# A hybrid encoder block: gate sums in two tiles, q and k weights split by halves of a head's dims, ropes without transfers

## The chip, the cores and the metric

The kernel runs on one core of a Trainium2 chip. The metric is the time of one execution on the device in microseconds (us). One execution was also recorded by the hardware profiler. The engines are TensorE (PE, its weight loads PEld), VectorE (DVE), ScalarE (ACT), GpSimd (POOL) and SyncE (SP), which here only issues transfers.

## The reference

One encoder block on 1024 tokens of width 1024, all in float32:

```
h    = rms_norm(x)
proj = h @ w_in                        # 1024 x 5120
qa, ka, va, qb, kb, vb, ga, gb = split(proj)
qa, ka, qb, kb = apply_rope(each)      # heads of 64 dims
ya = dilated_window_attention(qa, ka, va) @ w_branch_a
yb = differential_attention(qb, kb, vb) @ w_branch_b
x  = x + (sigmoid(ga) * ya + sigmoid(gb) * yb) @ w_out
x  = x + square(relu(rms_norm(x) @ w_ff1)) @ w_ff2
out = rms_norm(x)

def apply_rope(t):                     # per head, halves t1, t2 of 32 dims
    rot = concat([-t2, t1])
    return t * cos + rot * sin
```

What is computed here is q, k and the gates: 16 columns of 128 outputs for q and k (j = 0 to 15, two heads of 64 dims each) and 16 for the gates, out of `proj`.

## The kernel before

**Products.** Every float32 operand is split into a high and a low part (`halves`, L245 on ACT for the high part, L246 on POOL for the low), and a product takes three matmuls per block of the contraction: high by high, high by low, low by high. The projections go by the Strassen-Winograd form of a 2x2 block product: 7 products instead of 8, each of 12 matmuls of 128x512 (`product`, L237), with sums on the weights before (`rest_operands`, L265 to L268 on VectorE) and sums on the results behind (`rest_products`, L286 to L298). The blocks of the activations (B11, B21, B22, T1 to T4) lie split in SBUF.

**Stage 0** (to about 142 us) normalises and transposes x, forms v, and computes for four q/k pairs the first two of the 7 products (`qk_early`, `EARLY = (8, 12, 10, 14)`), which are parked in DRAM.

**Stage 1** (about 142 to 428 us) runs 16 tasks one behind the other: q8 g4 q12 g5 q10 g6 q14 g7 q0 g0 q4 g1 q2 q6 g2 g3. A q task (`qk_pair(j)`) forms the columns j and j + 1, a g task (`gate_rest(n)`) three quarters of two gate columns. An early q task and every gate task have 5 products here, the late q tasks (0, 4, 2, 6) 7. The products of a task stand in this order: s2 and s4 (into the PSUM tile y), s1 and s3 (into z), a4 (into "4"). The raw weights of a task are loaded two tasks ahead on SyncE's queue, 512 KB a tile. From them come three pairs of split tiles: ws (halves s2 and s4 of the first raw tile), wd (s1) and wt (s3 and a4 of the second). They take turns in three buffers (tags wh and wl), so a task's ws goes into the buffer of the ws of the task before, and so on; a late q task takes one more for its first two products (wa).

**Results and the rope.** A q task's sums go into two tiles of 128x1024, raw j and raw j + 1, of a tag "x" with four buffers. A gate task's three sums (gc0, gc1, gc2) take three buffers of the same tag and are stored to DRAM from SyncE's queue (`part_d`, gp in the trace, L539). The rope of a pair is emitted one task later, for j and then j + 1:

```
for b in range(4):                      # L493: swap the halves, 4 copies of 128 KB
    nc.sync.dma_start(rot[32*b:32*b+32, :], raw[32*(b^1):32*(b^1)+32, :])
rot = rot * scale * sin_t               # L494 VectorE
raw = raw * cos_t                       # L495 POOL
raw = raw * scale + rot                 # L496 VectorE
hi  = copy(raw)                         # L504 ACT
lo  = raw - hi                          # L505 VectorE
nc.scalar.dma_start(qk_d[j][0], hi)     # L506, on ACT's queue
nc.scalar.dma_start(qk_d[j][1], lo)     # L507
```

The column of a q/k tile holds two heads on 128 partitions, so the two halves of a head lie on different partitions.

**Order.** The code only says what depends on what. A scheduler sets the order of the instructions on each engine, and each engine (and each queue) then runs its list in that order. A tile's buffer is given on when the last instruction or transfer that uses it has ended. Behind stage 1 the attention phase takes the buffers of stage 1's ropes for its loads (kb and qb in the trace, L662 and L668), and its first statement on VectorE is a memset (L918) of a tile that lies where gate sums lay.

Of the kernel before, what the change touches and what calls it, by code (L numbers as in the profile page):

```python
# [37 lines left out]
def shape_tables():  # L38
# [8 lines left out]
    sin_t = np.concatenate([-sin, sin, -sin, sin], 0)  # L47
# [36 lines left out]
def tile_hybrid_block(ctx: ExitStack, tc: tile.TileContext, t: dict, out: bass.AP):  # L84
# [92 lines left out]
    qk_d = [dram(f"qk{j}", [2, P, S]) for j in range(16)]  # L177
# [84 lines left out]
    def rest_operands(name, ra, rb, s1):  # L262

        a11, a12, a21, a22 = ra[:, :DK, :], ra[:, DK:, :], rb[:, :DK, :], rb[:, DK:, :]
# [3 lines left out]
        nc.vector.tensor_tensor(a12, a12, a11, op=ALU.subtract)  # L268
        s2, s4 = halves(ra, f"ws_{name}")
# [248 lines left out]
    def qk_pair(j, raws):  # L518
# [5 lines left out]
        else:  # L524
            a11, a12 = halves(raws[0], f"wa_q{j}")
# [944 lines left out]
```

## Time and profile before

| | |
|---|---|
| time, median of 3 runs | 1668.82 us (1664.23 to 1673.82) |
| profiled execution | 1674.86 us, span 1673.1 us |
| busy: PE / DVE / ACT / POOL | 1557.9 / 1181.4 / 697.6 / 585.3 us (93 / 71 / 42 / 35%) |
| TensorE's granted clock over the span | 0.972 of 2.4 GHz |
| SyncE's queue / ACT's queue | 236.33 / 33.56 MB |
| transfers inside the rope | 64 of 128 KB, median 4.5 us to landing |
| q/k stores | 32 of 512 KB, median 4.8 us to landing |

The clock has two levels, 1.2 GHz (0.5) and 2.4 GHz (1.0); a stretch's mean lies between. A wait is put down to the engine, DMA or queue that released it last. An idle time in brackets stands on the instruction that ended it. PE is the busiest engine, so a gap of PE is what a change can take away, and a gap of another engine costs only where PE waits behind it.

### The profile page before, as it was taken

Reading aid. Unit: us, or ns where it says so; the run is one execution under the profiler, and the core shown is the slowest. Engines: PE = TensorE matmul, PEld = TensorE weight load, DVE = VectorE, ACT = ScalarE, POOL = GpSimd, SP = SyncE. Lnnn points to the kernel's source line nnn. Section 1 sums busy time; section 2 is a strip of 40 time slices with the busy share of each in tenths; the row PEclk is TensorE's granted clock in tenths of the full one; section 3 lists DMA queues with packets and bytes.
Section 4 is the critical chain, followed back from the end, with each engine's and each line's share of the span. In section 5 each row is a group of like instructions: output and inputs, shape, how many; then the busy total and the mean of one; then the engine's idle time right before and its main releaser. Section 6 shows DMA issues by size and latency. Waiting matters only on the chain. (4 is left out here: it accounts for less than half of the span.)

```text
span 1673.1 us, 20932 instructions
## 1 busy us (share of the span) xinstructions
PE 1557.9 (93%) x7832; PEld 1299.2 (78%) x7832; DVE 1181.4 (71%) x1367; ACT 697.6 (42%) x1064; POOL 585.3 (35%) x289
## 2 busy tenths in 40 slices
PE   8899889988789998989999999899999989999998
PEld 6798667766577887988887878687888867888776
DVE  5976798698688996645547357644355599898984
ACT  4432122232467774544433236444444552333331
POOL 1534444555232332012220003533333344354551
PEclk8999899998999999999999999999999999999999
DMA  6367566555767557656557333444333571423112
GB/s 214 125 210 215 164 196 223 175 184 163 263 194 233 200 191 271 204 180 215 156 162 278 110 130 94 120 128 130 114 101 101 179 268 51 163 74 116 51 38 101
DMA packets 214389, 271.23 MB, mean 162 GB/s; under 512 B 12784, under 2 KB 136848, under 8 KB 214288
## 3 DMA queue, kind: packets, MB, share of 16 engines
q1 hardware_dynamic: 200464, 236.33, 44.4%
q10 hardware_dynamic: 13824, 33.56, 5.3%
q8 instruction: 62, 1.02, 0.3%
q14 instruction: 39, 0.32, 0.1%
HBM read 183.81 MB, written 80.27 MB: 158 GB/s over the span
## 5 line engine op out<-in xcount | busy, mean ns | idle before, releaser
L1359 PE MATMUL p<-b,a 128*128 128x512 f32 x392 | 154.7, 395 | 5.1 <-DVE b L1274 5.1
L1358 PE MATMUL p<-b,a 128*128 128x512 f32 x392 | 154.2, 393 | 3.0 <-ACT a L1273 3.0
L1360 PE MATMUL p<-b,a 128*128 128x512 f32 x392 | 154.4, 396 | 2.0 <-DVE a L1274 1.9
L1274 POOL TENSOR_TENSOR b<-ws,b 128x1024 fp32r<-128x1024 f32 x20 | 61.4, 3088 | 95.3 <-ACT b L1273 85.3
L1359 PEld LDWEIGHTS p<-b,a 128*128 128x128 f32 x392 | 74.2, 189 | 23.0 <-DVE b L1274 6.0
L1274 POOL TENSOR_TENSOR b<-rb,b 128x1024 fp32r<-128x1024 f32 x21 | 70.8, 3390 | 54.7 <-ACT b L1273 46.7
L1360 PEld LDWEIGHTS p<-b,a 128*128 128x128 f32 x392 | 74.0, 189 | 20.1 <-DVE a L1274 3.9
L1358 PEld LDWEIGHTS p<-b,a 128*128 128x128 f32 x392 | 74.1, 189 | 19.8 <-ACT a L1273 3.4
L689 PE MATMUL sb<-kb,qb 128*128 128x512 f32 x256 | 74.7, 416 | 15.1 <-ACT p L694 8.8
L694 ACT ACTIVATE p<-sb,mn 128x1024 f32<-128x1024 f32 x64 | 71.3, 1116 | 38.5 <-DVE mn L692 23.7
L692 DVE TENSOR_REDUCE mn<-sb 128x1 f32<-128x1024 f32 x64 | 76.8, 1217 | 9.7 <-PE sb L689 9.2
L265 DVE TENSOR_TENSOR s<-w 128x512 f32<-128x512 f32 x15 | 16.2, 1081 | 85.8 <-DMA w<-in_w_ff 85.8
L156 POOL TENSOR_SCALAR n_y<-n_ss 128x1 f32<-128x1 f32 x23 | 5.1, 222 | 187.7 <-ACT n_xn L163 183.2
L803 PE MATMUL sa<-kh_a,zq 128*128 128x256 f32 x256 | 68.9, 300 | 1.2 <-DVE mna L812 1.2
L828 DVE TENSOR_TENSOR pta<-ta,pta 128x512 fp32r<-128x512 f32 x64 | 43.8, 688 | 33.9 <-ACT pta L827 33.7
L689 PEld LDWEIGHTS sb<-kb,qb 128*128 128x128 f32 x256 | 45.9, 192 | 27.9 <-ACT p L694 13.1
L1273 ACT ACTIVATE a<-fs 128x1024 fp32r<-128x1024 f32 x28 | 29.4, 1054 | 90.6 <-PE p L1359 71.3
L803 PE MATMUL sa<-kl_a,zq 128*128 128x256 f32 x256 | 65.8, 288 | 0.0
L246 POOL TENSOR_TENSOR wt_f_l<-w,wt_f_h 128x1024 fp32r<-128x1024 f32 x15 | 36.1, 2404 | 83.0 <-ACT wt_f_h L245 70.2
L816 ACT ACTIVATE sm<-sm,mna 128x512 f32<-128x512 f32 x64 | 46.1, 720 | 32.4 <-DVE mna L812 31.8
L827 ACT ACTIVATE pta<-ta 128x512 fp32r<-128x512 f32 x64 | 37.6, 591 | 52.2 <-PE ta L823 44.5
L1145 ACT ACTIVATE c<-c 128x512 f32<-128x512 f32 x64 | 39.9, 624 | 46.6 <-DVE c L292 34.9
(442 smaller groups left out, 4966.4 us busy)
## 6 DMA issues: line engine op xcount, KB each, us to landing
w<-in_w_in SPq DMA_DIRECT2D x32, 512.0 KB, 4.3
qk<-r ACTq DMA_DIRECT2D x32, 512.0 KB, 4.8
f<-c ACTq DMA_DIRECT2D x64, 256.0 KB, 2.0
rb<-in_w_ff SPq DMA_DIRECT2D x32, 512.0 KB, 4.6
ra<-f SPq DMA_DIRECT2D x64, 256.0 KB, 5.0
w<-in_w_ff SPq DMA_DIRECT2D x30, 512.0 KB, 4.2
vb<-vb SPq DMA_DIRECT2D x16, 512.0 KB, 6.6
rot<-raw SPq DMA_DIRECT2D x64, 128.0 KB, 4.5
```

The lines of the kernel that those rows point to most:

```text
L689: nc.tensor.matmul(sps[:, 512 * n:512 * n + 512], q[:, z, (qb % 4) * P:(qb % 4 + 1) * P], o.k[m][:, 512 * n:512 * n + 512], start=z == 0, ...
L692: nc.vector.tensor_reduce(mn, sps, axis=AX.X, op=ALU.min)
L694: nc.scalar.activation(p, sps, AF.Exp, scale=-1.0, bias=mn, accum_out=o.zz[qb][:, m:m + 1])
L803: nc.tensor.matmul(ps[:, 0:CM], zq[:, n % 4, c, :], kk[:, c * CM:(c + 1) * CM], start=c == 0 and kk is o.kh, stop=c == NCLS - 1 and kk is ...
L816: nc.scalar.activation(sm, sm, AF.Exp, scale=-1.0, bias=mn, accum_out=stat[h % 2][:, n:n + 1])
L827: nc.scalar.activation(view[0], tv, AF.Copy)
L828: nc.vector.tensor_tensor(view[1], tv, f(view[0]), op=ALU.subtract)
L1145: nc.scalar.activation(c, c, AF.Relu)
L1274: eng.tensor_tensor(lo, x, f(hi), op=ALU.subtract)
L1358: nc.tensor.matmul(acc, ah[:, i % 2, c], bh[:, i % 2, :], start=i == 0 and not more, stop=False, skip_group_check=bool(more))
L1359: nc.tensor.matmul(acc, ah[:, i % 2, c], bl[:, i % 2, :], start=False, stop=False, skip_group_check=bool(more))
L1360: nc.tensor.matmul(acc, al[:, i % 2, c], bh[:, i % 2, :], start=False, stop=last, skip_group_check=bool(more))
```

## The change

- The gate's sums take two tiles of "x" instead of three: gc0 holds two sums side by side, gc1 one.
- A q/k pair's weights are loaded as two tiles by halves of the contraction (rows 0 to 511 and 512 to 1023, 256 columns each). The 2x2 blocks of the product are now the first and second 32 dims of all four heads of the pair instead of its first and second column. So xa holds the first halves of four heads and xb the second halves, on the same partitions. The sums on the weights and the splits read and write views with runs of 32; ws holds s2 and s3, wt holds s4 and a4.
- The rope takes the pair at once, with no copies: two products on POOL, four instructions on VectorE, then the split of each tile; the low part goes into the tile that held the product with the sine.
- All q/k stores go out from SyncE's queue, into DRAM tiles of a pair (`qk_d`, 8 instead of 16), and the loads of the attention read them there.
- An early column is loaded as two tiles of 512 KB, of which half of the dims are used.

```diff
-    qk_d = [dram(f"qk{j}", [2, P, S]) for j in range(16)]
+    qk_d = [dram(f"qk{j}", [2, 2 * P, S]) for j in range(8)]
+
+    def qk_rows(j, half, z=slice(0, 2)):
+
+        r = 128 * (j % 2) + 64 * half
+        return qk_d[j // 2][z, r:r + 64, :]
...
-    def rest_operands(name, ra, rb, s1):
-
-        a11, a12, a21, a22 = ra[:, :DK, :], ra[:, DK:, :], rb[:, :DK, :], rb[:, DK:, :]
+    def rest_sums(a11, a12, a21, a22, s1):
+
         nc.vector.tensor_tensor(s1, a21, a22, op=ALU.add)
         nc.vector.tensor_tensor(a21, a11, a21, op=ALU.subtract)
         nc.vector.tensor_tensor(a11, s1, a11, op=ALU.subtract)
         nc.vector.tensor_tensor(a12, a12, a11, op=ALU.subtract)
+
+    def rest_operands(name, ra, rb, s1):
+        rest_sums(ra[:, :DK, :], ra[:, DK:, :], rb[:, :DK, :], rb[:, DK:, :], s1)
...
+    def qk_raw(j, name, slot):
+
+        return [v_raw_at(512 * k, qk_col(j), f"{name}{k}", *slot) for k in range(2)]
+
+    def v_raw_at(row, col, name, pool, tag, bufs):
+        r = pool.tile([P, DK, 256], F32, tag=tag, name=name, bufs=bufs)
+        nc.sync.dma_start(r, w_in[row:row + 512, col:col + 256].rearrange("(k p) n -> p k n", p=P))
+        return r
+
+    def qk_blocks(r):
+        x = r.rearrange("p k (h s i) -> p (k h) s i", s=2, i=32)
+        return [x[:, :, z, :] for z in range(2)]
+
+    def qk_first(raws, name, eng):
+        hi = wp.tile([P, DC, P], F32R, tag="wh", name=name + "_h", bufs=3)
+        lo = wp.tile([P, DC, P], F32R, tag="wl", name=name + "_l", bufs=3)
+        for k, r in enumerate(raws):
+            x = qk_blocks(r)[0]
+            to_hi, to_lo = [z[:, DK * k:DK * k + DK, :].rearrange("p k (h i) -> p (k h) i", i=32) for z in (hi, lo)]
+            nc.scalar.activation(to_hi, x, AF.Copy)
+            eng.tensor_tensor(to_lo, x, f(to_hi), op=ALU.subtract)
+        return [[z[:, DK * k:DK * k + DK, :] for z in (hi, lo)] for k in range(2)]
+
+    def qk_halves(r, name):
+
+        hi = wp.tile([P, DC, P], F32R, tag="wh", name=name + "_h", bufs=3)
+        lo = wp.tile([P, DC, P], F32R, tag="wl", name=name + "_l", bufs=3)
+        x = r.rearrange("p k (h s i) -> p (k h) s i", s=2, i=32)
+        to_hi, to_lo = [z.rearrange("p (s k) (h i) -> p (k h) s i", s=2, i=32) for z in (hi, lo)]
+        nc.scalar.activation(to_hi, x, AF.Copy)
+        nc.gpsimd.tensor_tensor(to_lo, x, f(to_hi), op=ALU.subtract)
+        return [[z[:, DK * a:DK * a + DK, :] for z in (hi, lo)] for a in range(2)]
...
-        a11, a12 = halves(col_raw(w_in, qk_col(EARLY[n]), f"wqe{n}", *SLOTS[n > 0]), f"wa_e{n}", nc.vector if n in (1, 2) else nc.gpsimd)
+        a11, a12 = qk_first(qk_raw(EARLY[n], f"wqe{n}", SLOTS[n > 0]), f"wa_e{n}", nc.vector if n in (1, 2) else nc.gpsimd)
...
-    def rope(j, raw):
+    def rope(j, xa, xb):
+
         scale = -0.125 if j % 8 < 4 else 1.0
-        rot = big("xn", f"rot{j}", 2)
-        for b in range(4):
-            o = b ^ 1
-            nc.sync.dma_start(rot[32 * b:32 * b + 32, :], raw[32 * o:32 * o + 32, :])
-        nc.vector.scalar_tensor_tensor(rot, rot, scale, sin_t, op0=ALU.mult, op1=ALU.mult)
-        nc.gpsimd.tensor_tensor(raw, raw, cos_t, op=ALU.mult)
-        nc.vector.scalar_tensor_tensor(raw, raw, scale, rot, op0=ALU.mult, op1=ALU.add)
-        hi, lo = [big("rh", f"r{z}_{j}", 2, F32R) for z in range(2)]
-        if j < 4:
-
-            src, to_hi, to_lo = [x.rearrange("p (a b j) -> p a b j", a=a, j=32) for x, a in ((raw, NCLS), (hi, NT), (lo, NT))]
-            to_hi, to_lo = [x.rearrange("p n c j -> p c n j") for x in (to_hi, to_lo)]
-        else:
-            src, to_hi, to_lo = raw, hi, lo
-        nc.scalar.activation(to_hi, src, AF.Copy)
-        nc.vector.tensor_tensor(to_lo, src, f(to_hi), op=ALU.subtract)
-        nc.scalar.dma_start(qk_d[j][0], f(hi))
-        nc.scalar.dma_start(qk_d[j][1], f(lo))
+        ta, tb = [big("xn", f"rot{j + z}", 2) for z in range(2)]
+        nc.gpsimd.tensor_tensor(tb, xb, sin_t, op=ALU.mult)
+        nc.vector.scalar_tensor_tensor(ta, xa, scale, sin_t, op0=ALU.mult, op1=ALU.mult)
+        nc.gpsimd.tensor_tensor(xb, xb, cos_t, op=ALU.mult)
+        nc.vector.scalar_tensor_tensor(xa, xa, scale, cos_t, op0=ALU.mult, op1=ALU.mult)
+        nc.vector.scalar_tensor_tensor(xa, tb, -scale, xa, op0=ALU.mult, op1=ALU.add)
+        nc.vector.scalar_tensor_tensor(xb, xb, scale, ta, op0=ALU.mult, op1=ALU.add)
+        for y, (raw, rot) in enumerate(((xa, tb), (xb, ta))):
+            hi, lo = big("rh", f"r{y}_{j}", 2, F32R), rot.bitcast(F32R)
+            if j < 4:
+
+                src, to_hi, to_lo = [x.rearrange("p (a b j) -> p a b j", a=a, j=32) for x, a in ((raw, NCLS), (hi, NT), (lo, NT))]
+                to_hi, to_lo = [x.rearrange("p n c j -> p c n j") for x in (to_hi, to_lo)]
+            else:
+                src, to_hi, to_lo = raw, hi, lo
+            nc.scalar.activation(to_hi, src, AF.Copy)
+            nc.vector.tensor_tensor(to_lo, src, f(to_hi), op=ALU.subtract)
+            for z, x in enumerate((hi, lo)):
+                nc.sync.dma_start(qk_d[j // 2][z].rearrange("(h s i) t -> s h i t", s=2, i=32)[y], f(x))
...
-            a11, a12 = halves(raws[0], f"wa_q{j}")
+            a11, a12 = qk_first(raws, f"wa_q{j}", nc.gpsimd)
             first_products(f"q{j}", a11, a12, p, xa[:, 0:512])
-        operands = rest_operands(f"q{j}", *raws, s1_tile(f"q{j}"))
-        rest_products(f"q{j}", operands, p, u, (xa[:, 512:], xb[:, :512], xb[:, 512:]), lambda *_: None)
-        return lambda: (rope(j, xa), rope(j + 1, xb))
+        (a11, a21), (a12, a22) = [qk_blocks(r) for r in raws]
+        s1 = s1_tile(f"q{j}")
+        rest_sums(a11, a12, a21, a22, s1.rearrange("p k (h i) -> p (k h) i", i=32))
+        s2, s3 = qk_halves(raws[0], f"ws_q{j}")
+        (s1,) = halves(s1, f"wd_q{j}", nc.vector)
+        s4, a4 = qk_halves(raws[1], f"wt_q{j}")
+        rest_products(f"q{j}", (s1, s2, s3, s4, a4), p, u, (xa[:, 512:], xb[:, :512], xb[:, 512:]), lambda *_: None)
+        return partial(rope, j, xa, xb)
...
-        dst = [p1.tile([P, 512], F32, tag="x", name=f"gc{n}{k}", bufs=4) for k in range(3)]
+        two, one = [big("x", f"gc{n}{k}", 4) for k in range(2)]
+        dst = two[:, 0:512], one[:, 0:512], two[:, 512:1024]
...
-            nc.sync.dma_start(f(k), qk_d[12 + h][:, 64 * m:64 * m + 64, :].rearrange("z d s -> d z s"))
+            nc.sync.dma_start(f(k), qk_rows(12 + h, m).rearrange("z d s -> d z s"))
```

On VectorE, around the rope of the pair 8 and 9 and the sums of gate 4 (w1_2x and w1_3x: raw weights of the next tasks, yg4, zg4 and 4g4: the gate's products). Before:

```order
127 L246 TENSOR_TENSOR wd_q12_l_1734<-s1_q12_1724,wd_q12_h_1733 128x512
128 L494 SCALAR_TENSOR_TENSOR rot8_1690<-rot8_1690,sin_t_1478 128x1024
129 L292 TENSOR_TENSOR gc40_1594<-zg4_1615,gc40_1594 128x512
130 L294 TENSOR_TENSOR gc41_1595<-zg4_1615,gu4_1593 128x512
131 L496 SCALAR_TENSOR_TENSOR raw8_1497<-raw8_1497,rot8_1690 128x1024
132 L505 TENSOR_TENSOR r1_8_1699<-raw8_1497,r0_8_1698 128x1024
133 L295 TENSOR_TENSOR gc42_1596<-zg4_1615,gc41_1595 128x512
134 L298 TENSOR_TENSOR gc41_1595<-4g4_1616,gc41_1595 128x512
135 L494 SCALAR_TENSOR_TENSOR rot9_1704<-rot9_1704,sin_t_1478 128x1024
```

Now:

```order
122 L536 SCALAR_TENSOR_TENSOR rot8_1697<-raw8_1505,sin_t_1486 128x1024
123 L272 TENSOR_TENSOR w1_20_1597<-s1_q12_1721,w1_20_1597 128x16x32
124 L538 SCALAR_TENSOR_TENSOR raw8_1505<-raw8_1505,cos_t_1485 128x1024
125 L540 SCALAR_TENSOR_TENSOR raw9_1506<-raw9_1506,rot8_1697 128x1024
126 L539 SCALAR_TENSOR_TENSOR raw8_1505<-rot9_1698,raw8_1505 128x1024
127 L297 TENSOR_TENSOR gc40_1602<-yg4_1621,gu4_1601 128x512
128 L273 TENSOR_TENSOR w1_21_1599<-w1_21_1599,w1_20_1597 128x16x32
129 L550 TENSOR_TENSOR rot9_1698<-raw8_1505,r0_8_1705 128x1024
130 L550 TENSOR_TENSOR rot8_1697<-raw9_1506,r1_8_1710 128x1024
131 L252 TENSOR_TENSOR wd_q12_l_1731<-s1_q12_1721,wd_q12_h_1730 128x512
132 L300 TENSOR_TENSOR gc40_1602<-zg4_1622,gc40_1602 128x512
133 L302 TENSOR_TENSOR gc41_1603<-zg4_1622,gu4_1601 128x512
```

Before, the two ropes stand among the gate's z sums (L292 to L298) one after the other; now the pair's rope stands ahead of them in one piece, ahead of the y sum (L297) as well.

On TensorE, in the task of q12 (yq12, zq12: its PSUM tiles; hT and hB: blocks of the activations). Before:

```order
906 L237 MATMUL yq12_1741<-hT20_181,ws_q12_h_1729 128x512
907 L237 MATMUL yq12_1741<-hT21_182,ws_q12_h_1729 128x512
908 L237 MATMUL yq12_1741<-hT20_181,ws_q12_l_1730 128x512
...
918 L237 MATMUL yq12_1741<-hB220_177,ws_q12_h_1729 128x512
919 L237 MATMUL yq12_1741<-hB221_178,ws_q12_h_1729 128x512
920 L237 MATMUL yq12_1741<-hB220_177,ws_q12_l_1730 128x512
...
942 L237 MATMUL zq12_1742<-hT30_183,wt_q12_h_1737 128x512
943 L237 MATMUL zq12_1742<-hT31_184,wt_q12_h_1737 128x512
944 L237 MATMUL zq12_1742<-hT30_183,wt_q12_l_1738 128x512
```

Now:

```order
906 L243 MATMUL yq12_1738<-hT20_173,ws_q12_h_1726 128x512
907 L243 MATMUL yq12_1738<-hT21_174,ws_q12_h_1726 128x512
908 L243 MATMUL yq12_1738<-hT20_173,ws_q12_l_1727 128x512
...
918 L243 MATMUL yq12_1738<-hB220_169,wt_q12_h_1734 128x512
919 L243 MATMUL yq12_1738<-hB221_170,wt_q12_h_1734 128x512
920 L243 MATMUL yq12_1738<-hB220_169,wt_q12_l_1735 128x512
...
942 L243 MATMUL zq12_1739<-hT30_175,ws_q12_h_1726 128x512
943 L243 MATMUL zq12_1739<-hT31_176,ws_q12_h_1726 128x512
944 L243 MATMUL zq12_1739<-hT30_175,ws_q12_l_1727 128x512
```

The second product now reads wt, and the fourth reads ws.

On SyncE's queue, at the end of stage 1 (gp2 and gp3: the stores of the last gates' sums, kb0 and qb0: the first attention loads, qk3: the pair 6 and 7). Before:

```order
154 L539 DMA gp2_1483<-gc22_3184 128x512
155 L622 DMA gq4_3490<-gp4_1485 128x2x512
156 L539 DMA gp2_1483<-gc21_3183 128x512
157 L662 DMA kb0_0_3425<-qk12_84 128x1x1024
158 L662 DMA kb0_1_3427<-qk12_84 128x1x1024
159 L668 DMA qb0_0_0_3429<-qk8_80 128x1x512
160 L539 DMA gp3_1484<-gc30_3303 128x512
161 L668 DMA qb0_0_0_3429<-qk8_80 128x1x512
162 L539 DMA gp3_1484<-gc32_3305 128x512
163 L539 DMA gp3_1484<-gc31_3304 128x512
164 L668 DMA qb0_1_0_3432<-qk8_80 128x1x512 x2
165 L668 DMA qb0_0_1_3435<-qk8_80 128x1x512 x2
```

Now:

```order
166 L552 DMA qk3_75<-rot6_3213 4x32x1024
167 L590 DMA gp2_1491<-gc20_3122 128x512
168 L257 DMA wgf4_3412<-in_w_in 128x8x128
169 L590 DMA gp2_1491<-gc20_3122 128x512
170 L590 DMA gp2_1491<-gc21_3123 128x512
171 L720 DMA kb0_0_3353<-qk6_78 128x1x1024
172 L720 DMA kb0_1_3355<-qk6_78 128x1x1024
173 L726 DMA qb0_0_0_3357<-qk4_76 128x1x512 x2
174 L726 DMA qb0_1_0_3360<-qk4_76 128x1x512 x2
175 L726 DMA qb0_0_1_3363<-qk4_76 128x1x512 x2
176 L726 DMA qb0_1_1_3366<-qk4_76 128x1x512 x2
177 L590 DMA gp3_1492<-gc30_3232 128x512
```

The first attention loads now stand ahead of all stores of gate 3, behind the rope's last stores and those of gate 2.

## Rows read from the trace of the kernel before

**Rows 1.** Windows: start and end, length, busy time (instructions) by engine, clock, DMA, GB/s

```profile
142.00:428.00 286.00, 260.98 (x1057) 203.74 (x1058) 231.72 (x214) 71.03 (x81) 139.75 (x52) 0.95 0.61 192
177.00:200.00 23.00, 16.28 (x59) 12.79 (x58) 18.12 (x20) 4.76 (x5) 8.33 (x3) 0.78 0.75 245
213.00:250.00 37.00, 32.30 (x135) 24.60 (x134) 33.63 (x32) 9.07 (x10) 15.61 (x8) 1.00 0.67 207
402.00:428.00 26.00, 24.94 (x97) 19.51 (x96) 24.16 (x20) 7.85 (x9) 13.32 (x5) 0.88 0.66 218
428.00:450.00 22.00, 12.76 (x47) 8.64 (x45) 9.32 (x13) 6.46 (x12) 4.12 (x4) 0.84 0.83 274
```

**Rows 2.** Timeline of PE: start, length, engine, line, operation [idle before <-releaser]

```profile
171.54 0.62 PE L237 MATMUL yq<-hT,ws_q_h 128*128 128x512 f32 x2
174.34 0.62 PE L237 MATMUL yq<-hB,ws_q_h 128*128 128x512 f32 x2
```

**Rows 3.** Waits, 141.9 to 440 us: total, times, longest

```profile
PE zq L237 <- DVE gc L295: 7.5, 2, 6.7
PE zg L237 <- DVE raw L295: 5.2, 3, 4.1
PE yq L237 <- POOL ws_q_l L246: 2.5, 2, 1.8
PE sb L689 <- DMA qb<-qk: 6.3, 1, 6.3
```

**Rows 4.** Timeline of ACT, POOL and VectorE around one gate's sums

```profile
171.55 1.06 ACT L245 ACTIVATE wt_q_h<-w 128x1024 fp32r<-128x1024 f32 x1 [4.96 <-PE 4g L237]
...
172.69 2.73 POOL L246 TENSOR_TENSOR wt_q_l<-w,wt_q_h 128x1024 fp32r<-128x1024 f32 x1 [2.61 <-ACT wt_q_h L245]
179.85 2.34 POOL L495 TENSOR_TENSOR raw<-raw,cos_t 128x1024 f32<-128x1024 f32 x1 [4.43 <-DMA rot<-raw]
...
179.95 3.32 DVE L505 TENSOR_TENSOR r<-raw,r 128x1024 fp32r<-128x1024 f32 x1 [1.12 <-ACT r L504]
```

**Rows 5.** Groups, 150 to 450 us; last, one tile's row with shortest, median, longest ns

```profile
L494 DVE SCALAR_TENSOR_TENSOR rot<-rot,sin_t 128x1024 f32<-128x1024 f32 x16 | 24.1, 1509 | 2.6 <-DMA rot<-raw 2.6
L495 POOL TENSOR_TENSOR raw<-raw,cos_t 128x1024 f32<-128x1024 f32 x16 | 44.1, 2760 | 22.2 <-DMA rot<-raw 12.3 <-PE yq L237 5.6 <-DVE gc L289 3.2
L496 DVE SCALAR_TENSOR_TENSOR raw<-raw,rot 128x1024 f32<-128x1024 f32 x16 | 34.1, 2132 | 2.7 <-POOL raw L495 2.3
L505 DVE TENSOR_TENSOR r<-raw,r 128x1024 fp32r<-128x1024 f32 x16 | 30.5, 1906 | 6.9 <-ACT r L504 4.9 <-DMA qk<-r 2.0
L504 ACT ACTIVATE r<-raw 128x1024 fp32r<-128x1024 f32 x16 | 17.0, 1061 | 78.9 <-DVE raw L496 78.9
...
L246 POOL TENSOR_TENSOR wt_q_l<-w,wt_q_h x8: 2395/2772/3437, 144.5 to 375.1; 128x1024 fp32r<-128x1024 f32 x8
```

**Rows 6.** Timeline from the stage to the attention; last, a DMA group of 380:440

```profile
424.04 0.33 ACTq L507 DMA_DIRECT2D qk<-r  x1
...
428.00 1.26 SPq L662 DMA_DIRECT2D kb<-qk  x2
...
428.00 0.69 DVE L298 TENSOR_TENSOR gc<-4g,gc 128x512 f32<-128x512 f32 x1
437.62 0.31 DVE L918 MEMSET stat<- 128x128 f32 x2 [8.92 <-DMA gp<-gc]
...
gp<-gc SPq DMA_DIRECT2D x6, 256.0 KB, 5.7
```

**Rows 7.** DMA issues of the page; then the timeline of PE

```profile
w<-in_w_in SPq DMA_DIRECT2D x32, 512.0 KB, 4.3
...
77.70 1.22 PE L237 MATMUL f1e<-hB,wa_e_h 128*128 128x512 f32 x2 [3.16 <-DVE s_ec L260]
```

**Rows 8.** Timeline of PE in the task of q6

```profile
372.28 0.74 PE L237 MATMUL yq<-hT,ws_q_h 128*128 128x512 f32 x2 [0.78 <-ACT ws_q_h L245]
374.82 0.79 PE L237 MATMUL yq<-hT,ws_q_l 128*128 128x512 f32 x1 [1.81 <-POOL ws_q_l L246]
```

More of the change, by code (lines that the diff above doesn't have):

```diff
@@ L46, in shape_tables @@
     cos_t = np.concatenate([cos] * 4, 0)
-    sin_t = np.concatenate([-sin, sin, -sin, sin], 0)
+    sin_t = np.concatenate([sin] * 4, 0)
     def additive(count):
@@ L541, in gate_rest, with gate_raw @@
         rest_products(f"g{n}", rest_operands(f"g{n}", *raws, s1_tile(f"g{n}")), None, u, dst, done)
+    def gate_raw(n, name, slot):
+        return [col_raw(w_in, 3072 + 256 * n + P * a, f"{name}{a}", *slot) for a in range(2)]
     GATES = (4, 5, 6, 7, 0, 1, 2, 3)
@@ L545, in tile_hybrid_block, with load_raws @@
     for j, n in zip(EARLY + (0, 4, 2, 6), GATES):
-        todo += [(partial(qk_pair, j), qk_col(j)), (partial(gate_rest, n), 3072 + 256 * n)]
+        todo += [(partial(qk_pair, j), partial(qk_raw, j)), (partial(gate_rest, n), partial(gate_raw, n))]
     todo = todo[:13] + todo[14:15] + todo[13:14] + todo[15:]
-    raws = [raw_pair(w_in, todo[n][1], f"w1_{n}", SLOTS) for n in range(2)]
+    def load_raws(n):
+        turn1[0] ^= 1
+        return todo[n][1](f"w1_{n}", SLOTS[turn1[0]])
+    raws = [load_raws(n) for n in range(2)]
     ropes = []
@@ L552, in tile_hybrid_block @@
         if n + 2 < len(todo):
-            raws.append(raw_pair(w_in, todo[n + 2][1], f"w1_{n + 2}", SLOTS))
+            raws.append(load_raws(n + 2))
         if n == 8:
@@ L592, in load_qk @@
     def load_qk(jq, jk, half, name):
-        r = slice(64 * half, 64 * half + 64)
-        q_src = qk_d[jq][:, r, :].rearrange("z d s -> d z s")
+        q_src = qk_rows(jq, half).rearrange("z d s -> d z s")
         k_src = [bass.AP(tensor=a.tensor, offset=a.offset, ap=[[S, 64], [0, 2], [1, S]])
-                 for a in (qk_d[jk][0, r, :], qk_d[jk][1, r, :])]
+                 for a in (qk_rows(jk, half, 0), qk_rows(jk, half, 1))]
         tiles = []
@@ L668, in b_open @@
                     nc.sync.dma_start(
-                        f(q)[:, z, :], dup(qk_d[8 + h][z, 64 * m:64 * m + 64, 512 * half:512 * half + 512]))
+                        f(q)[:, z, :], dup(qk_rows(8 + h, m, z)[:, 512 * half:512 * half + 512]))
                 o.q[m, half] = q
```

## The prediction

> **What bounds the kernel now.** I read the windows first. In the stage that is changed (142 to 428 us) TensorE is busy 260.98 of 286 us and the mean granted clock is 0.95, while VectorE is busy 231.72, POOL 139.75 and ACT 71.03 [rows 1]: TensorE sets the time there, and what can be won is its idle time and the time at the lower clock level. How much that is comes from one product: 12 matmuls, which start at 171.54 and are followed by the next product at 174.34, so 2.80 us at the full clock [rows 2]. The stage holds 8 q/k tasks (5 products each, 7 in the four late ones) and 8 gate tasks of 5, 88 products: 88 x 2.80 = 246.4 us. The stage takes 286, so 39.6 us are lost: 286 - 260.98 = 25.0 of them idle, some 14.6 at 1.2 GHz.
>
> The waits of TensorE say for whom. The largest are VectorE's sums of a gate (L295, 7.5 us) and of a q/k pair (L295, 5.2 us), then POOL's low part of a weight half (ws_q_l, 2.5 us); after the stage 6.3 us go to the first attention load [rows 3]. Behind both L295 waits stands the rope. In the first (the gate's sum) three sums ask for buffers of a tag that has four, two of them held by the pair that is being roped, so the third stands in VectorE's list behind the rope's last subtraction (L505), which was running from 179.95 to 183.27 when TensorE stood [rows 4]. In the second (a pair's sum, late in the stage) VectorE is simply behind with its list, rope instructions among it: it is busy 24.16 of 26 us from 402 to 428 [rows 1]. Both stretches lose the clock too: 177 to 200 has a mean of 0.78, which is 2 x 0.22 x 23 = 10.1 us at the low level, and 402 to 428 has 0.88, 6.2 us [rows 1]; work at half speed loses half of it, 5.0 and 3.1.
>
> **The change part by part.** The sum is made against the profiled execution, 1674.86 us, which is 6.0 above the median of 1668.82.
>
> *Two tiles for the gate's sums.* Two raws and two sums fill the four buffers, so no sum waits for a rope that is still going on; the next pair's raws take the buffers of the pair two tasks back. Now the rope stands in one piece ahead of the z sums; with the 12.5 us worked out below it is done some 4 us before the next task asks for the bank. That takes away the first wait and its clock, 7.5 + 5.0 = 12.5. Of the second and its clock, 5.2 + 3.1 = 8.3, I take three quarters, 6.2, since the late pairs' ropes also stand in one piece, but VectorE's load is the same. -18.7; all would be -20.8, and nothing if POOL holds the rope up and the sums with it.
>
> *The rope without transfers.* The 64 copies between partitions go, and with them whatever waited for them. VectorE's instructions stay 6 per pair and POOL's 2 per pair (now on the second half, L535 and L537). The rope's work is 24.1 + 34.1 + 30.5 = 88.7 us on VectorE and 44.1 on POOL before [rows 5], and I book the same after. So VectorE's load does not change, only the time from a pair's last sum to the free buffers: two POOL products of 2.76, a 2.13 us sum, an ACT copy of 1.06 and two subtractions of 1.91 are about 12.5 us, under the 14 us of a gate's five products. It is off TensorE's path, booked at nothing; its cover is gone if POOL is late, and then the next pair's first sum waits.
>
> *The strided views.* ACT's copy of 128x1024 takes 1061 ns on average over 16, four of which already write runs of 32 through a four-level view [rows 5]; were those four half as slow again, the mean would stand 12% higher. I book nothing for ACT and VectorE. POOL is not shown on such views: between the median of 2772 ns and the 3437 that wt_q_l took once I take the first; the other end is 0.7 us for each of 15 halves, 10 us at most.
>
> *The order of the products.* The split by halves of a head's dims puts s2 and s3 in one half tile (ws) and s4 and a4 in the other (wt). A q/k task now wants wt at its second product, and keeps ws until its fourth. wt is written into the buffer that the gate's last product read. In the trace that product ended by 171.54, ACT's high part ran from 171.55, POOL's low part from 172.69 to 175.42 [rows 4]; the second product's low matmul stands 0.47 behind 174.34, at 174.8 [rows 2]. So 0.6 us late with this pair, 0.3 with POOL's quickest (2.40) and 1.3 with its slowest (3.44) [rows 5]: I take 0.85 for 7 tasks, 6.0. The same holds one task on: ws of the next gate goes into the buffer that is free after the fourth product, and needs 1.06 + 2.74 and the hand-over, while one product of 2.80 and the two high matmuls (0.47) lie between: 0.55 late, 8 times, 4.4. Before, it had three products' time. These 10.4 us are new. I book no clock for them: between 213 and 250 TensorE was idle for 4.7 us in pieces and the granted clock stayed at 1.00 [rows 1].
>
> *The stores on SyncE's queue.* ACT no longer stands behind L505 to issue them. The loads of the next pair stand ahead of the stores of a rope for gates, behind them for pairs. No large wait of TensorE is for sums on weights [rows 3]; nothing is booked. If a store holds a pair's load back, the sum s1 needs both tiles, and the whole task starts late.
>
> *The first attention load.* It has to wait for the last rope's store to have read its tile, since it takes its place: the store was issued at 424.04, the load at 428.00 [rows 6], and TensorE stood 6.3 us. Now ropes 6 and 7 end inside the next-to-last gate, and the load follows the sums of that gate, some 14 us earlier. What is late next is VectorE's memset, which waits for the last gate's sums to be stored: it started at 437.62, since the stores were issued among the attention loads, while the sum itself was done at 428.7. The stores now stand behind those loads, long issued by then; with 5.7 us to landing the memset comes at 434.4, 3.2 us earlier [rows 6]. I take -3.2; the ends are 0 and the whole wait with its clock (0.84 from 428 to 450, 7.0 us at the low level, 3.5 lost), -9.8.
>
> *The early loads.* Each early column is now two loads of 512 KB into both buffers, so the last waits until both halves of the one before are split. Such a load lands in 4.3 us, and POOL's split follows. But the last early product waited 3.16 us for a bank before it started at 77.70 [rows 7], which swallows most of a delay. +1.5, from 0 to +6.
>
> Sum: -18.7 + 6.0 + 4.4 - 3.2 + 1.5 = -10.0, so 1664.9 for the profiled execution and 1658.8 against the median; I say 1658.
>
> **The rivals.** B: *VectorE's list is what TensorE waits for, whatever the buffers.* For it: 231.7 of 286 us busy, and L505 stands before L295 in the list. Against it: from 213 to 250 it was busy 33.63 of 37 us and TensorE still got 32.3. Then the stage keeps its length and -3.2 + 1.5 is left: 1667.
>
> C: *the new stalls don't come*, since POOL takes its shortest time when no rope runs beside it, and the wait for ws_q_l goes too: -20.8 - 2.5 - 3.2 = -26.5, 1642. Against it: POOL's means were measured in this very stage.
>
> D, slower: *the short stalls let the clock fall.* After a wait of only 0.78 us at 372.28 two matmuls took 0.74 us instead of the 0.62 of [rows 2], and a single one at 374.82 took 0.79 [rows 8], which is the low level. It decides from the point where the 15 stalls are near the upper end (1.3 us, 19.5 in place of 10.4) and every third one brings 7 us at 1.2 GHz, as after the stage, 3.5 lost, 17.5 in all: -10.0 + 9.1 + 17.5 = +16.6, 1685. Against it: the stretch from 213 to 250.
>
> E: *the rope's work slows down.* L505 took 3.32 us at 179.95, beside a POOL product that began at 179.85 [rows 4], against a mean of 1.91. If all 48 rope instructions of VectorE met a POOL product, they would take 48 x 3.32 = 159.4 us instead of 88.7, 70.7 more, where VectorE has 286 - 231.7 = 54.3 idle: the stage would be 16.4 longer, 1683 with the other terms. Against it: POOL's time does not grow (44.1 for its 16 products), and only what lies beside it is stretched. The Trainium skill (GPSIMD Engine Reference, Key points) says that POOL shares its SBUF interfaces with VectorE and contends with instructions that read two SBUF inputs; the trace agrees with the sharing by the 3.32 and shows no pair of the new kind.
>
> **How the numbers follow.** A (forecast) 0.44, B 0.24, C 0.12, D 0.14, E 0.06. A's own range is 1649 to 1668. For the 8 in 10 I go from near C to near D and E, 1640 to 1683, which also holds the unknown ends (POOL's views +10, the early loads +6, the transition -9.8). 0.5% of the median, 8.3 us, is what a measurement can tell here: faster means under 1660.5, slower over 1677.2. Faster: 0.29 of A, all of C and 0.05 of B, 0.46; slower: D, E and 0.02 of B, 0.22; within: 0.32.
>
> **What would show it.** Right: no TensorE wait on L303 (the sum that was L295) over 1 us, granted clock near 1.00 through the early pairs, and the first attention matmul within a microsecond or two of the last gate. The new stalls should appear as TensorE waiting for wt_q_l (POOL) and ws_g_l, 0.3 to 1.4 us each. Wrong: TensorE still waiting for a sum while a rope instruction of VectorE runs (B), low clock behind the short stalls (D), rope instructions of VectorE over 2.5 us on average (E), or a weight load that lands after its sum was due, since SyncE stood at a store.

## The result, and the profile after

The changed kernel takes 1782.26 us (median of 4 runs, 1777.48 to 1782.55) where the kernel before takes 1666.93 with one more run: 1.0672 times as long, 95% interval 1.0647 to 1.0696 (the ratio on record; the quotient of the two medians is 1.069). The forecast was 1658 and the range ended at 1683.

Where the time went is read from three marks, taken from the timelines of TensorE: the start of the first product of the pair 8 and 9, the end of the last gate's last product, and the first transposition of the attention that follows.

| us | before | after |
|---|---|---|
| stage starts | 141.91 | 144.65 |
| its last product ends | 427.81 | 519.79 |
| first transposition | 446.80 | 552.57 |
| end of the profiled execution | 1674.86 | 1782.41 |

An end here is the start of the last matmul and 0.24, the step from one matmul to the next. In the changed kernel a gap follows it:

```profile
519.55 0.40 PE L243 MATMUL 4g<-hT,wt_g_l 128*128 128x512 f32 x1
533.52 0.76 PE L747 MATMUL sb<-kb,qb 128*128 128x512 f32 x1 [13.57 <-DMA qb<-qk]
```

Of the 107.55 us between the two executions the stage has 375.14 - 285.90 = 89.2, the transition from its end to the first transposition 32.78 - 18.99 = 13.8, the start 2.7 and everything behind the 1.8 that remain. The stage as one window answers to [rows 1] (columns as there):

```profile
144.65:519.79 375.14, 280.40 (x1056) 216.02 (x1056) 220.62 (x210) 68.98 (x83) 144.12 (x55) 0.86 0.38 119
```

TensorE stands for 375.14 - 280.40 = 94.7 us, 69.7 more than before, and works 19.4 us longer on the same products, with the mean granted clock at 0.86 in place of 0.95. VectorE and ACT are no busier (220.62 and 68.98 us), POOL by some 4 us (144.12). The waits of 140 to 520 us answer to [rows 3] (engine, tile and line, releaser: total, times, longest):

```profile
DVE s_q L270 <- DMA w<-in_w_in: 72.5, 6, 22.8
PE zg L243 <- DVE raw L303: 36.4, 4, 15.2
DVE s_g L270 <- DMA w<-in_w_in: 24.0, 2, 15.3
PE yg L243 <- DVE raw L297: 23.9, 2, 15.9
```

TensorE waits for VectorE's sums, as it did before, but VectorE now waits for weights: 96.5 us for the loads that feed the sums of weights, where the same two groups had 18.6 us in the kernel before (140 to 440 us):

```profile
DVE s_g L265 <- DMA w<-in_w_in: 15.8, 5, 6.8
DVE s_q L265 <- DMA w<-in_w_in: 2.8, 2, 1.5
```

The first rope shows the order of events. SyncE's queue in the changed kernel, issue instructions with start, length, line and transfer:

```profile
178.38 0.55 SPq L552 DMA_DIRECT2D qk<-rot  x1
...
181.16 1.89 SPq L552 DMA_DIRECT2D qk<-r  x1
...
186.15 1.74 SPq L552 DMA_DIRECT2D qk<-rot  x1
187.99 3.61 SPq L590 DMA_DIRECT2D gp<-gc  x1
191.64 1.51 SPq L568 DMA_DIRECT2D qp<-qe  x1
...
194.59 2.97 SPq L447 DMA_DIRECT2D w<-in_w_in  x2
```

And VectorE and TensorE in the same stretch:

```profile
207.72 0.69 DVE L296 TENSOR_TENSOR qu<-yq,qp 128x512 f32<-128x512 f32 x1 [21.72 <-DMA qp<-qe]
208.44 0.69 DVE L297 TENSOR_TENSOR raw<-yq,qu 128x512 f32<-128x512 f32 x1
```

```profile
209.28 1.19 PE L243 MATMUL yg<-hT,ws_g_h 128*128 128x512 f32 x2 [15.91 <-DVE raw L297]
```

Four stores of a rope go out from 177 to 188; the load of qp, 256 KB, is issued at 191.64 and has landed only by 207.7. VectorE's list stands 21.72 us at the sum that wants qp, the PSUM bank it would free comes 15.91 us late for TensorE, and the clock is at 1.2 GHz when it starts again (1.19 us for two matmuls, 0.62 in [rows 2]). Before, a 512 KB load landed in 4.3 us [rows 7]. What lies between is seen best where little but stores is under way, behind the last rope but one (windows of the changed kernel; a weight load lands by 480.6; the last two columns are the mean busy share of the 16 DMA engines and GB/s):

```profile
480.00:484.00 4.00, 2.81 (x13) 1.92 (x11) 3.24 (x5) 0.00 (x0) 0.00 (x0) 1.00 0.26 107
484.00:488.00 4.00, 1.93 (x5) 1.58 (x6) 2.61 (x5) 0.00 (x0) 1.20 (x1) 0.60 0.25 103
```

A quarter of the engines' time, steadily: as much as 4 of 16 engines would have; the view gives only the mean of the 16. A store's DRAM side is now the view `s h i t` of 4 x 32 x 1024, with the four heads outermost. At 105 GB/s the 2 MB of one pair (four stores of 512 KB) take 20 us, an estimate, and the loads that follow are late. The last rope shows the same at the stage's end: its four stores are issued from 500.50 to 505.08, the first attention load, which takes over a buffer of the ropes, not before 526.47, and TensorE stands for the 13.57 us above.

### The profile page after: what moved, and what is told of

It is laid out like the page before. It is cut to its first block, busy times and chain, and to the rows that moved or that the text cites. A ratio compares the mean times of both kernels' runs of the same rounds, so it can differ in the third digit from the quotient of the medians.

```text
span 1780.6 us, 20825 instructions
## 1 busy us (share of the span) xinstructions
PE 1582.2 (89%) x7832; PEld 1313.6 (74%) x7832; DVE 1177.6 (66%) x1369; ACT 699.0 (39%) x1072; POOL 579.5 (33%) x295
## 5 line engine op out<-in xcount | busy, mean ns | idle before, releaser
L1332 POOL TENSOR_TENSOR b<-rb,b 128x1024 fp32r<-128x1024 f32 x21 | 64.3, 3081 | 62.8 <-ACT b L1331 62.8
L750 DVE TENSOR_REDUCE mn<-sb 128x1 f32<-128x1024 f32 x64 | 76.7, 1216 | 12.1 <-PE sb L747 11.5
L270 DVE TENSOR_TENSOR s<-w 128x512 f32<-128x512 f32 x15 | 18.0, 1199 | 84.1 <-DMA w<-in_w_ff 84.1
L549 ACT ACTIVATE r<-raw 128x1024 fp32r<-128x1024 f32 x16 | 16.5, 1055 | 129.2 <-DVE raw L539 121.7
L243 PE MATMUL zg<-hT,wd_g_h 128*128 128x512 f32 x64 | 26.9, 512 | 36.4 <-DVE raw L303 36.4
```

Of the source, the lines that this page charges most:

```text
L243: nc.tensor.matmul(acc, w[wz][:, k, :], hb[nm][hz][:, k, :], start=k == 0 and wz + hz == 0, stop=k == DK - 1 and wz == 1)
L750: nc.vector.tensor_reduce(mn, sps, axis=AX.X, op=ALU.min)
L1332: eng.tensor_tensor(lo, x, f(hi), op=ALU.subtract)
```

## The experiments

**What the stores cost.** Theory: the outermost size of the DRAM view sets on how many DMA engines a store runs. Rival: SyncE's queue is the wrong place for them, whatever their shape. Two kernels change only the view, and with it in which DRAM rows q and k lie (alike for both, so that q times k is the same); every engine's instructions stay as they are. Two more put the stores back on ACT's queue, in either shape.

```
rows16:     qk_d[j // 2][z].rearrange("(p s) t -> s p t", s=2)[y]             (128 x 1024, every second row)
groups8:    qk_d[j // 2][z].rearrange("(g s i) t -> s g i t", g=8, s=2)[y]    (8 x 16 x 1024)
act4:       -nc.sync.dma_start(...)  +nc.scalar.dma_start(...)                (4 x 32 x 1024, as in the changed kernel)
rows16_act: rows16, issued by nc.scalar
```

> The changed kernel, with the two halves of a head's dims interleaved row by row in DRAM, so that a q/k store's DRAM side is 128 rows instead of 4 x 32 rows; every engine's list is the same as in the changed kernel, same bytes. T1 (the stores are slow: with 4 outermost they run on 4 of the 16 DMA engines, and what stands behind them waits): the plateaus of DMA share 0.2 at 100 GB/s vanish, no wait of VectorE for qp or weights over 5 us, time 1650 to 1675. T2 (the place of the stores in SyncE's list: a store waits for its rope, and the loads behind it come late): 1765 to 1790, as the changed kernel.

> As rows16, but the DRAM side of a store is 8 groups of 16 rows; every engine's list the same, same bytes. T1: plateaus of DMA share near 0.45 and about 200 GB/s while stores run, half as long as in the changed kernel, and most of the loss gone since a pair's 2 MB then take some 10 us: 1660 to 1710. T2: 1765 to 1790.

> The changed kernel with all q/k stores (still 4 x 32 rows) issued from ACT's queue. T1: the loads no longer stand behind the stores in one queue but share four DMA engines with them, plateaus of 0.2 stay: 1690 to 1760. T2: the loads are free: 1650 to 1675.

> rows16 with the stores issued from ACT's queue. T1: within 0.5% of rows16. T2: 1650 to 1675, over 100 us faster than rows16.

| kernel | us | against before, 95% |
|---|---|---|
| changed (4 outermost) | 1782.26 | 1.0672 [1.0647, 1.0696] |
| act4 | 1769.65 | 1.0598 [1.0571, 1.0625] |
| groups8 | 1714.54 | 1.0271 [1.0245, 1.0297] |
| rows16 | 1682.50 | 1.0084 [1.0057, 1.0111] |
| rows16_act | 1683.88 | 1.0087 [1.0064, 1.0110] |

The dose is there: 4, 8, 128 rows outermost give 1.067, 1.027, 1.008. Three of the four missed the theory's range on the slow side: rows16 by 7.5 us, groups8 by 4.5, act4 by 9.7. So act4's theory had the place of the stores in the queue worth more than it is; no rival's range was met.

The share of the DMA engines follows, in the windows behind the same rope of groups8:

```profile
424.00:428.00 4.00, 4.00 (x19) 3.23 (x18) 0.47 (x1) 1.06 (x1) 0.00 (x0) 1.00 0.52 193
428.00:432.00 4.00, 3.75 (x17) 2.67 (x15) 3.84 (x7) 0.00 (x0) 0.00 (x0) 1.00 0.50 207
```

and of rows16:

```profile
399.00:403.00 4.00, 4.00 (x19) 3.23 (x18) 2.30 (x4) 1.06 (x1) 0.87 (x1) 1.00 0.98 293
403.00:405.00 2.00, 2.00 (x11) 1.59 (x10) 2.00 (x1) 0.63 (x1) 1.53 (x1) 1.00 1.03 420
```

SyncE's queue at the first rope in rows16, beside the one above:

```profile
182.00 0.38 SPq L552 DMA_DIRECT2D qk<-r  x1
...
184.72 0.42 SPq L552 DMA_DIRECT2D qk<-rot  x1
...
185.92 0.73 SPq L568 DMA_DIRECT2D qp<-qe  x1
...
187.44 1.00 SPq L447 DMA_DIRECT2D w<-in_w_in  x2
```

The same list, but the weights are issued 7 us earlier and land in 4.3 (the median of its page). The first window of rows16 holds a weight load of 512 KB beside the stores, and that of groups8 the end of one, which VectorE has at 427.53; the second windows hold stores alone. There the rates are 103, 207 and 420 GB/s, near 1 to 2 to 4 (a share of 1.03 is full, within what the view resolves). The rival falls: with whole rows both queues give the same time, and with four outermost ACT's queue keeps VectorE waiting as long (`DVE s_q L270 <- DMA w<-in_w_in: 69.8, 6, 17.6`). So slow stores hold up the loads whichever queue issues them; the queue is worth 0.7% with slow stores and nothing with quick ones.

Two more kernels ask whether it is the DRAM rows or the shape of the transfer. groups16 has 16 x 8 x 1024. four_stores writes exactly the rows of the changed kernel, each store cut into four of 32 rows:

```
groups16:    rearrange("(g s i) t -> s g i t", g=16, s=2)[y]
four_stores: for h in range(4):
                 r = 64 * h + 32 * y
                 nc.sync.dma_start(qk_d[j // 2][z][r:r + 32, :], f(x)[32 * h:32 * h + 32, :])
```

> As groups8, but the DRAM side of a store is 16 groups of 8 rows; every engine's list the same, same bytes. Theory (number of DMA engines by the outermost count, at most 16): as rows16 within 0.5%, 1674 to 1691. Rival (the groups themselves slow the store: short runs of rows): no faster than groups8, 1710 or more.

> The changed kernel with its DRAM layout, each q/k store cut into four of 32 rows (128 KB), so that 32 stands outermost on both sides instead of 4. Theory (number of DMA engines by the outermost count): near rows16, 1675 to 1695, as 128 issues of some 0.4 us fit SyncE's idle time. Rival (what counts in rows16 is the layout of the rows in DRAM, or SyncE's list): 1700 or more.

groups16: 1683.85, 1.0109 [1.0080, 1.0138], the time of rows16. four_stores: 1698.26, 1.0198 [1.0164, 1.0232]. With the same bytes in the same DRAM rows as the changed kernel it is some 79 us quicker (1.0672 - 1.0198), so the addresses can account for no more of the loss than what is left. It stays about 1.1% above rows16, 3 us over the theory's range and 2 short of the rival's; it issues 128 stores in place of 32, 2.15 us for four in one row of its SyncE queue, and the lists of the engines differ too. What of the 1.1% is which was not tried.

The transfers themselves, as groups of 140 to 520 us (count, KB each, median us from issue to landing), of groups16:

```profile
qk<-r SPq DMA_DIRECT2D x16, 512.0 KB, 5.1
qk<-rot SPq DMA_DIRECT2D x16, 512.0 KB, 5.6
```

and of rows16:

```profile
qk<-r SPq DMA_DIRECT2D x16, 512.0 KB, 3.4
qk<-rot SPq DMA_DIRECT2D x16, 512.0 KB, 3.0
```

Some two microseconds more for a store (1.7 and 2.6) cost nothing that shows; the loads behind it still come in time.

**The sums in two tiles.** This was the largest term, -18.7. Once alone in the kernel before, and once taken out of rows16:

```
two_tiles:   before, with the two lines `two, one = ...` and `dst = two[:, 0:512], one[:, 0:512], two[:, 512:1024]` for its three tiles
three_tiles: rows16, with the three tiles of before for these two lines
```

> The kernel before with one edit: the gate's sums in two tiles. Theory of the prediction (the third buffer made the gate's sum wait for the rope): the wait of TensorE for L295 of a gate (7.5 us) goes, with the clock that it costs: 7 to 19 us faster than before, 1648 to 1661. Rival (VectorE's list is behind anyway): 1663 to 1673.

> rows16 with the gate's sums back in three tiles. Theory after two_tiles (that edit alone is worth nothing, since the wait moves in VectorE's list): within 0.7% of rows16, 1671 to 1694. Rival (with the rope in one piece the third buffer would wait for its end): 8 us or more slower, over 1691.

two_tiles: 1668.77, 1.0022 [1.0002, 1.0042]. three_tiles: 1679.85, 1.0082 [1.0059, 1.0105], as rows16. Without the edit or with it the time is the same within 0.5%: the term is nothing. The waits of TensorE in two_tiles, 140 to 450 us:

```profile
PE zg L237 <- DVE raw L295: 8.6, 6, 2.6
PE zq L237 <- DVE gc L295: 5.1, 2, 3.5
```

The long wait of 6.7 us for the gate's sum is gone, as forecast, but both groups together still hold 13.7 us where [rows 3] had 12.7: the wait has moved to other places of the same list. That is rival B's mechanism.

**What is left with quick stores.** In rows16 the stage runs from 145.39 to 441.15, 295.8 us with 260.34 busy: the clock (0.96) is as before, TensorE idles 10.4 us more. Its waits from 145 to 442 us:

```profile
PE yq L243 <- DVE gc L297: 11.5, 3, 4.8
PE yq L243 <- POOL wt_q_l L471: 11.2, 7, 5.3
PE zg L243 <- POOL wt_g_l L252: 6.5, 4, 2.0
```

The second was forecast, at half the size. The first was not, and VectorE's list shows it (rows16, up to the gate's first sum, L297, for which TensorE stood 4.76 us at 212.97):

```profile
200.48 3.43 DVE L536 SCALAR_TENSOR_TENSOR rot<-raw,sin_t 128x1024 f32<-128x1024 f32 x1
203.84 2.89 DVE L273 TENSOR_TENSOR w<-w,w 128x512 f32<-128x512 f32 x1
206.65 3.40 DVE L538 SCALAR_TENSOR_TENSOR raw<-raw,cos_t 128x1024 f32<-128x1024 f32 x1
209.97 1.21 DVE L540 SCALAR_TENSOR_TENSOR raw<-raw,rot 128x1024 f32<-128x1024 f32 x1
211.10 1.21 DVE L539 SCALAR_TENSOR_TENSOR raw<-rot,raw 128x1024 f32<-128x1024 f32 x1
212.24 0.68 DVE L297 TENSOR_TENSOR gc<-yg,gu 128x512 f32<-128x512 f32 x1
```

and POOL beside it:

```profile
200.03 2.80 POOL L535 TENSOR_TENSOR rot<-raw,sin_t 128x1024 f32<-128x1024 f32 x1 [2.43 <-DVE raw L306]
202.91 3.26 POOL L537 TENSOR_TENSOR raw<-raw,cos_t 128x1024 f32<-128x1024 f32 x1
206.14 2.83 POOL L471 TENSOR_TENSOR ws_q_l<-w,ws_q_h 128x1024 fp32r<-128x1024 f32 x1
```

While POOL works, VectorE's rope instruction takes 3.4 us, and a 128x512 difference 2.89 in place of some 0.7; once POOL is through, at 208.97, a rope instruction takes 1.21. It is not POOL alone that holds up the other. At the next rope VectorE begins first:

```profile
235.38 1.21 DVE L536 SCALAR_TENSOR_TENSOR rot<-raw,sin_t 128x1024 f32<-128x1024 f32 x1
235.53 3.33 POOL L535 TENSOR_TENSOR rot<-raw,sin_t 128x1024 f32<-128x1024 f32 x1 [2.43 <-DVE raw L306]
236.62 3.33 DVE L538 SCALAR_TENSOR_TENSOR raw<-raw,cos_t 128x1024 f32<-128x1024 f32 x1
```

There L536 keeps its 1.21 and POOL's product has 3.33 in place of 2.80; then L538 ends 1.09 us behind the end of that product, as L536 above ended 1.08 behind POOL's. In these rows the one that begins later ends about its own time behind the other, as if it stood until then; no run tests that.

The whole rope stands ahead of L297 in the list.

Three kernels follow. wt_later orders the products of a q/k task as s2, s1, s3, s4, a4, so that wt is wanted at the fourth (both sums into the bank of y, then z). y_first puts the rope's last two sums, which wait for POOL, behind the gate's first sum. both is the two together. All stand on rows16.

```
wt_later: +product(b6, s2, "T2"); product(b5, s1, "T1"); ...; product(b7, s3, "T3"); product(b3, s4, "B22"); ...; product(b4, a4, "T4")
y_first:  +first_sum[0] = nc.vector.tensor_tensor(c12, b3, u, op=ALU.add)
          +with tc.issue_after(first_sum[0].ins):
          +    rope_sums(xa, xb, ta, tb, scale)      (L539 and L540 of before this edit)
```

> rows16 with the products of a q/k task in the order s2, s1, s3, s4, a4 (each PSUM tile still given on after two products, five sums as before), so that wt is wanted at the fourth product again, not the second. Theory (the split of the weights by dims made wt late): TensorE's waits for wt_q_l (11.2 us in 7 cases in rows16) vanish, 8 to 20 us faster than rows16: 1663 to 1675. Rival (VectorE's or POOL's list is what is late, and the wait comes at the next place): within 0.5% of rows16, 1674 to 1691.

> rows16 with the two instructions of the rope on VectorE that wait for POOL queued behind the first sum of the next gate (L297, the y sum). Theory (the y sum stands behind a rope that waits for POOL): TensorE's waits for the gate's L297 (14.6 us in 4 cases in rows16) fall under 5, 8 to 18 us faster than rows16: 1665 to 1675. Rival (the rope is then late for its buffers and the next pair waits): within 0.5% of rows16, 1674 to 1691.

> rows16 with both edits, wt_later and y_first. If both terms are separate: the sum of the two gains, 1648 to 1664. If one of them only hands its wait to the other: no faster than the better of the two.

wt_later: 1686.55, 1.0117 [1.0092, 1.0141]; y_first: 1674.93, 1.0055 [1.0036, 1.0074]; both: 1666.76, 1.0004 [0.9991, 1.0017]. Against rows16, in per cent: +0.33, -0.29 and -0.79; the intervals of the first two overlap with that of rows16, that of both does not. The trace of wt_later has no large wait for wt_q_l left and y_first's waits for the y sum fell to 3.5 us, as their theories said, but the gains did not follow: wt_later lies in the rival's range, y_first at 1674.93 in both of its ranges, and both between its two cases, 2.8 us above the sum of the gains and 8 below the better single one. The two do not add: each alone leaves the other's wait, and it grows (in wt_later the wait for L297 from 11.5 to 13.7, with 10.3 new ones for VectorE's wd_q_l; in y_first the wait for wt_q_l from 11.2 to 14.6). With both, no wait of the stage is over 6.2 in total, 140 to 450 us:

```profile
PE zq L243 <- DVE gc L305: 6.2, 3, 2.6
```

and the stage takes 282.2 us (to 427.4), 3.7 less than before. It starts at 145.25, 3.3 later, which takes most of that back. At the first transposition the profiled execution of both is 2.4 us ahead of the one of before (444.38 and 446.80), and the medians are the same; one kernel's executions differ by more (1662.65 to 1669.29 for both), so where the rest goes stays open.

**The early loads.** early_half is both, with each early column loaded as the half that is wanted (four loads of 128x8x32 into one buffer) and not in full:

```
+for h in range(4):
+    c = qk_col(j) + 64 * h
+    nc.sync.dma_start(r[:, :, 32 * h:32 * h + 32], w_in[:, c:c + 32].rearrange("(k p) i -> p k i", p=P))
```

> The kernel of both, with an early column loaded as its 32 wanted dims per head alone (four loads of 128 KB into one buffer, 128 bytes a run) instead of two loads of 512 KB into two buffers. Theory (the early loads start the stage 3.3 us late: 145.25 in both against 141.91 before): the stage starts by 142.5 and the time is 3 to 6 us under both, 1660 to 1664, 0.1 to 0.4% under before. Rival (the stage waits for the last sums of v, whose wait stands in front of it in both kernels): within 2 us of both.

1660.68, 0.9963 [0.9943, 0.9983] against before. The start of the stage in both:

```profile
145.25 1.19 PE L243 MATMUL yq<-hT,ws_q_h 128*128 128x512 f32 x2 [2.23 <-DVE vc L443]
```

and in early_half:

```profile
138.53 0.71 PE L243 MATMUL yq<-hT,ws_q_h 128*128 128x512 f32 x2 [2.05 <-DVE vc L443]
```

6.7 us earlier, and at the higher clock; the first transposition of the attention comes 6.8 earlier (437.6 after 444.4). That is twice the 3.3 us that the theory spoke of, and the clock has a part in it: from 60 to 140 us the mean granted clock is 0.96 in early_half and 0.91 in both, which is some 4 us of 80, an estimate. The edit also splits a column in one piece where both takes two, and which of the two counts was not tried. Nor is it shown why the stage starts 3.4 us ahead of the kernel before, whose early columns are as many bytes. This version is 0.37% quicker than the kernel before, and with it than the changed one.

## Why the prediction was wrong, step by step

**The step that failed** is "The stores on SyncE's queue", booked at nothing. It asked where the stores stand in the queue and found no wait that hung on it; that a store has become another transfer was not asked. It stood in the piece of SyncE's list ahead of the prediction, `qk3_75<-rot6_3213 4x32x1024` beside loads of 128 rows. Its price is 1.0672 - 1.0084 = 0.0588 of 1667, some 98 us. The way it came is the one that step's last sentence and "what would show it" name, a weight load that lands after its sum was due; it had no rival of its own and so no price. The cover, "no large wait of TensorE is for sums on weights", was read from stores that landed in 4.8 us (`qk<-r` in the page of before), and on TensorE alone: VectorE's own waits for loads, 15.8 us in five pieces up to 6.8, already said that the loads come with little room.

By the rows above, stores with 4 outermost have a quarter of the engines' time, with 8 half of it, and whole rows all. The Trainium skill (DMA: Bandwidth & Descriptors, Why a DMA increments its semaphore by 16 and not by 1) states this as a rule: a copy is split over the largest number, at most 16, that divides the slowest dimension, other than 1, of both sides. The shares of 0.25, 0.50 and 1.03 agree with it for 4, 8 and 128. By it, as a rival, the stores could have been priced: a pair's 2.1 MB at a quarter of the 274 GB/s of [rows 1] are 30.6 us, an estimate, and more than the 28 that TensorE needs for a pair's task and a gate's, 10 products of 2.80. At the measured 105 GB/s it is 20 us, less than the 28, and the loads came late all the same.

**Two tiles for the gate's sums**, -18.7: nothing, shown by two_tiles and three_tiles. The buffer did hold the sum back, but behind it stood a list of VectorE's that was as late elsewhere. The argument against B, a stretch in which VectorE was 33.63 of 37 us busy and TensorE ran, was from another stretch of the list.

**The order of the products**, +10.4: the waits came at the right place for wt_q_l, 7 times as forecast, 11.2 us in place of 6.0. For ws of the next gate none came (no ws_g row among TensorE's waits of rows16); wt_g_l took 6.5 in its stead. In sum 17.7. For wt_q_l the working held but for one case, 5.30 of the 11.2:

```profile
387.44 3.21 POOL L537 TENSOR_TENSOR raw<-raw,cos_t 128x1024 f32<-128x1024 f32 x1
390.61 3.32 POOL L471 TENSOR_TENSOR wt_q_l<-w,wt_q_h 128x1024 fp32r<-128x1024 f32 x1
393.98 0.80 PE L243 MATMUL yq<-hB,wt_q_l 128*128 128x512 f32 x1 [5.30 <-POOL wt_q_l L471]
```

ACT's high part ended at 386.27, but both products of a rope (the first at 384.51) stood ahead of wt_q_l in POOL's list, which the working did not look at. The other six waits (0.20 to 2.04) make 5.9, where 6.0 was booked for seven.

**The rope without transfers**, 0: its cover, "done some 4 us before the next task asks" (under the two tiles), did not hold where POOL held VectorE up. The rope stands ahead of the y sum too, as the order ahead of the prediction shows, and the working looked at the z sums alone (11.5 us). Rival E had the mechanism, not its size. Groups of rows16, 145 to 442 us, answer to [rows 5]:

```profile
L538 DVE SCALAR_TENSOR_TENSOR raw<-raw,cos_t 128x1024 f32<-128x1024 f32 x8 | 24.4, 3056 | 0.2
L550 DVE TENSOR_TENSOR rot<-raw,r 128x1024 fp32r<-128x1024 f32 x16 | 22.4, 1418 | 0.5 <-ACT r L549 0.5
L539 DVE SCALAR_TENSOR_TENSOR raw<-rot,raw 128x1024 f32<-128x1024 f32 x8 | 19.8, 2477 | 0.4
L540 DVE SCALAR_TENSOR_TENSOR raw<-raw,rot 128x1024 f32<-128x1024 f32 x8 | 19.4, 2431 | 11.5 <-POOL raw L537 11.5
L536 DVE SCALAR_TENSOR_TENSOR rot<-raw,sin_t 128x1024 f32<-128x1024 f32 x8 | 16.4, 2045 | 0.0
```

102.4 us, 13.7 more than the 88.7 of before, where E had 70.7, and 2.13 on average, under the 2.5 that E named as its sign (its 1683 leaves out the -18.7 and the +10.4; with all terms its sum is 1675). POOL's 16 products took 51.7 in place of 44.1, which E's counter-argument had excluded. That VectorE had room on average did not help the sum that stood behind.

**The strided views**, 0: right. In rows16 the mean of ACT's rope copies is 1056 ns, and of its copies of the weights 1052 and 1061.

**The first attention load**, -3.2: the wait of 6.3 us for it is gone and the first attention matmul of rows16 follows the last product without a gap, but the time from there to the first transposition is 18.7 us, against 19.0 before. The memset came 7.8 us behind the stage's end where it had been 9.8; 5.99 us now go to one later wait, `sb` for ACT's p, at 452.44. So -0.3. In the changed kernel itself, with its slow stores, that wait is not gone but 13.57 us.

**The early loads**, +1.5: +3.5 (rows16 starts its stage at 145.39 where before started at 141.91), and 6.7 between both and early_half, clock included.

Rows16's sum by its own trace is 3.5 + 9.9 - 0.3 = 13.1, and the measured ratio gives 14.0. That they agree so well is luck in part: the profiled execution of before was 6.0 above its median, and behind the first transposition it took 6.8 us longer than that of rows16. D did not come: in rows16 the clock of the stage is 0.96 with these stalls.

## What to carry to other kernels

When a change gives a transfer another view, read its shape in the list of DMAs as well as its place: with 4, 8 and 128 outermost on the DRAM side the same stores ran at 103, 207 and 420 GB/s here, and a slow store was paid for by the loads behind and beside it, on either queue. A wait that is freed in an in-order list is worth no more than the next instruction of that list that is late, so test such a term alone. Average room on an engine says nothing about the one sum for which the next engine stands.

## What was not expected of the hardware

- Stores with 4 outermost moved 103 to 107 GB/s at a DMA share of 0.25 to 0.26; with 8, 193 to 207 at 0.50 to 0.52; with 128 rows 420 at 1.03.
- Behind such stores SyncE's issue instructions themselves got longer: 1.74 to 1.89 us for a store and 3.61 for a gate's store, against 0.38 to 0.42 and 0.32 in rows16 at the same place.
- Beside a 128x1024 product of POOL, VectorE's 128x1024 instructions that began later took up to 3.4 us instead of 1.21 and a 128x512 one 2.89 instead of 0.7; the one that began first kept its 1.21, and POOL's product took 3.33 (means of 3141 and 3324 ns in rows16, 2760 in [rows 5]).
